# Convolution taps summed by accumulating transfers, and more seven-product chunk pairs in the up projection

## The chip, the cores and the metric

The kernel runs on one core of one Trainium2 chip. The metric is device time in microseconds: the median of three runs, 2211.19 us (2211.04 to 2212.21). The engines are TensorE (PE; PEld is its weight load), VectorE (DVE), ScalarE (ACT), GpSimd (POOL) and SyncE (SP, which here only issues transfers). Each works through its own queue in order, and they wait for each other by semaphores. Sixteen DMA engines move the data.

## The reference

Two decoder layers on one sequence of 256 tokens and width 2048 in float32; the first mixes by gated linear attention, the second by forgetting attention, and both read 256 memory tokens. Behind each mixer stands the channel mixer that this change concerns:

```python
def causal_dwconv(u, w, b):
    s_ = u.shape[1]
    up = jnp.pad(u, ((0, 0), (CONV_WIDTH - 1, 0), (0, 0)))
    return w[0] * up[:, 0:s_] + w[1] * up[:, 1:s_ + 1] + w[2] * up[:, 2:s_ + 2] + b

def conv_ffn(h, w_up, conv_w, conv_b, w_down):
    u = causal_dwconv(h @ w_up, conv_w, conv_b)
    a, val = split_cols(u, [FFN_HIDDEN, FFN_HIDDEN])
    return (jax.nn.silu(a) * val) @ w_down
...
    for i in range(DEPTH):
        ...
        h = rmsnorm(x, norm_ffn[i])
        x = x + conv_ffn(h, ffn_w_up[i], ffn_conv_w[i], ffn_conv_b[i], ffn_w_down[i])
    return rmsnorm(x, norm_final)
```

`FFN_HIDDEN` is 5632, so `w_up` is 2048 x 11264 and `w_down` 5632 x 2048; the convolution has three taps along the tokens.

## The kernel before

**Products in parts.** Every weight chunk of 128 x 1024 values is loaded as float32 (`raw`, four buffers), cast on ScalarE to a high part (`whi`, four buffers), and VectorE subtracts to get the low part (`wlo`, four buffers). The activations (`h`, in bufA and bufB) are held as two parts as well. A product is three matmuls: both activation parts with the high weights, and the high activations with the low weights. Casts and subtractions are issued with raised priority (`AHEAD`), so the scheduler, which orders all engines by a simulated time line, puts them well ahead of the matmuls.

**The channel mixer** (`ffn`). The up projection runs in 11 panels for each layer, `j` = 0, 4, ..., 40: four blocks of 128 channels of the gate half and the same four of the value half. A panel walks 16 chunks of the input dimension (`pair_steps`): four products of 128 tokens x 512 channels in a chunk, 12 matmuls of 512 columns. Two neighbouring chunks `k`, `k+1` that stand in `sums` are computed together by a scheme of seven products in place of eight, 21 matmuls in place of 24. It takes two loads into `raw2`, four sums of weight halves on VectorE (L437 to L440), and four casts and subtractions (L382, L383: one of 512 columns and three of 1024), and it uses sums over tokens of the input, prepared once a layer (`up_sums`). All panels take the pair of chunks 6 and 7. Panels whose number stands in `MORE_IN` take the pair of chunks 11 and 12 (`SEVEN_MORE`) as well: panels 5, 6 and 8. After up panels 0 to 4, 5 to 7 and 8 to 10 follow down projections (`down_pair`), of the same build.

**From panel to product.** When a panel's banks are complete, `turn` transposes its result on VectorE into `y` (tile `yu` or `yzu`), two slots to a panel. Through GpSimd's queue it is stored to DRAM (`far`, L650) and fetched back as four pieces (L655, into `fvt` or `yzu`), which brings channels onto partitions. Then for each slot: twelve ScalarE instructions scale the result by the taps' weights (`tap_of`, L1414; tap 0 with the bias), into three tiles `taps[0..2]` that both slots share; two VectorE instructions add taps 1 and 2 to tap 0 (`add_tap`, L1421); ScalarE applies SiLU in place (`silu`, L1427); VectorE multiplies gate and value (`gated`, L1434) and the product is split into parts for the down projection.

**What sets their place.** This work is cut into steps, each with a cost and a due time, in one list `waiting`. `tick` is called once for each chunk step; it gives credit (1.45 a step, 1.7 in panels of `MORE_IN`) and takes steps in order while credit lasts and they are due. A panel's results come back three ticks after its end, and its steps are due after seven or eight.

## Time and profile before

| | before |
|---|---|
| median of three runs | 2211.19 us |
| span of the profiled execution | 2210.2 us |
| own time of the profiled execution, beyond its span | not given |
| mean granted TensorE clock | 0.999 |
| first to last convolution tap, layer 0 | 517.7 to 1118.6 us |
| first to last convolution tap, layer 1 | 1556.2 to 2155.8 us |
| DMA, mean over the span | 233 GB/s |

The profile shows one execution. "Busy" is the time in which an engine works, as a share of the span. A group row reads: line, engine, operation, output<-inputs by the program's names, shapes and count | busy us, mean ns of one | idle time of the engine just before them and what ended it. Matmuls are pipelined, so the mean of one matmul is longer than the time from one to the next; the chain's time over its count is the pace.

### The profile page before, as it was taken

The numbers are of one execution on the slowest core, as the hardware profiler recorded it, in microseconds if no ns is written. First come the engines' busy times: TensorE is split into PE (matmuls) and PEld (weight loads), VectorE is DVE, ScalarE is ACT, GpSimd is POOL, SyncE is SP. The second block draws the span as 40 slices with busy tenths as digits, with TensorE's granted clock in tenths as the row PEclk, the third lists the DMA queues.
The fourth block names the chain that finished last, engine by engine and source line by source line (L and its number), as shares of the span: only waits on it lengthen the run. The fifth ranks groups of instructions, "written<-read, shape, count | busy, mean of one in ns | idle before, by whom it ended". The sixth has DMA issues, their size and how long they took to land.

```text
span 2210.2 us, 30065 instructions
## 1 busy us (share of the span) xinstructions
PE 2199.2 (100%) x10315; PEld 1851.8 (84%) x10315; DVE 1793.1 (81%) x2655; ACT 1421.8 (64%) x2260; POOL 136.5 (6%) x257
## 2 busy tenths in 40 slices
PE   9999999999999999999999999999999999999998
PEld 7888888888888888888888998888888888888886
DVE  7768977688897889888978669668888888988896
ACT  6655664566787567656865555555788656765874
POOL 0000000001100000001110000000100000100100
PEclk9999999999999999999999999999999999999999
DMA  9867567777677567667678767677777657776774
GB/s 343 259 224 224 190 194 236 252 232 253 227 243 265 187 219 233 231 234 247 222 244 265 231 201 243 225 239 241 228 241 248 234 187 237 243 247 224 227 259 153
DMA packets 166289, 515.41 MB, mean 233 GB/s; under 512 B 20780, under 2 KB 42552, under 8 KB 166136
## 3 DMA queue, kind: packets, MB, share of 16 engines
q1 hardware_dynamic: 149064, 460.99, 63.1%
q0 software_dynamic: 16496, 51.71, 7.5%
q8 instruction: 81, 1.33, 0.2%
q10 hardware_dynamic: 576, 0.79, 0.1%
q14 instruction: 72, 0.59, 0.1%
HBM read 469.62 MB, written 43.79 MB: 232 GB/s over the span
## 4 chain that ended last, share of the span: by engine, by line
PE 99%; DVE 1%; ACT 0%; issue 0%; DVEq 0%; ACTq 0%
PE acc L412 29%; PE acc L338 26%; PE ps_s L412 15%; PE ps_o L412 8%; PE ps_t L412 7%; PE acc L309 3%; PE acc L264 3%; PE ps_s L338 2%; PE acc L368 2%; PE acc L262 1%; PE ps_s L1035 0%; PE ps_o L701 0%; PE ps_s L701 0%; PE ps_s L1308 0%; PE ps_s L1081 0%; PE ps_o L1263 0%
## 5 line engine op out<-in xcount | busy, mean ns | idle before, releaser
L234 DVE TENSOR_TENSOR wlo<-raw,whi 128x1024 fp32r<-128x1024 f32 (+2 forms) x705 | 841.2, 1203 | 241.3 <-ACT whi L233 220.7
L233 ACT ACTIVATE whi<-raw 128x1024 fp32r<-128x1024 f32 (+2 forms) x705 | 729.8, 1046 | 405.4 <-PE acc L338 131.9
L338 PE MATMUL acc<-whi,B 128*128 128x512 f32 (+3 forms) x1248 | 291.7, 370 | 0.0
L382 ACT ACTIVATE whi<-raw 128x1024 fp32r<-128x1024 f32 (+1 forms) x144 | 137.0, 954 | 197.4 <-PE acc L412 75.4
L338 PEld LDWEIGHTS acc<-whi,B 128*128 128x128 f32 x1248 | 226.8, 188 | 28.1
L412 PE MATMUL acc<-whi,mix 128*128 128x512 f32 x756 | 192.9, 389 | 0.0
L412 PE MATMUL acc<-whi,B 128*128 128x512 f32 x738 | 189.8, 389 | 0.0
L383 DVE TENSOR_TENSOR wlo<-raw,whi 128x1024 fp32r<-128x1024 f32 (+1 forms) x144 | 156.2, 1089 | 40.3 <-ACT whi L382 37.2
L412 PEld LDWEIGHTS acc<-whi,mix 128*128 128x128 f32 x756 | 141.9, 188 | 29.5
L412 PEld LDWEIGHTS acc<-whi,B 128*128 128x128 f32 x738 | 138.5, 188 | 28.7
L338 PE MATMUL acc<-wlo,B 128*128 128x512 f32 (+3 forms) x624 | 158.5, 369 | 0.0
L338 PEld LDWEIGHTS acc<-wlo,B 128*128 128x128 f32 x624 | 114.5, 188 | 14.6
L1414 ACT ACTIVATE tap<-fvt,cw 128x256 f32<-128x256 f32 x264 | 123.5, 531 | 2.6 <-DMA fvt<-far 2.5
L1414 ACT ACTIVATE tap<-yzu,cw 128x256 f32<-128x256 f32 x264 | 123.5, 531 | 2.0 <-DMA yzu<-far 2.0
L1421 DVE TENSOR_TENSOR tap<-tap,tap 128x1024 f32<-128x1024 f32 x88 | 107.2, 1219 | 1.4 <-ACT tap L1414 1.0
L412 PE MATMUL ps_s<-whi,mix 128*128 128x512 f32 x386 | 106.2, 389 | 0.0
L412 PE MATMUL acc<-wlo,mix 128*128 128x512 f32 x378 | 105.6, 389 | 0.0
L412 PE MATMUL acc<-wlo,B 128*128 128x512 f32 x369 | 105.1, 389 | 0.0
L412 PE MATMUL ps_s<-whi,B 128*128 128x512 f32 x342 | 93.1, 389 | 0.0
L412 PEld LDWEIGHTS ps_s<-whi,mix 128*128 128x128 f32 x386 | 72.5, 188 | 15.0
L412 PEld LDWEIGHTS acc<-wlo,mix 128*128 128x128 f32 x378 | 70.9, 188 | 14.7
L412 PEld LDWEIGHTS acc<-wlo,B 128*128 128x128 f32 x369 | 69.3, 188 | 14.4
(502 smaller groups left out, 3866.5 us busy)
## 6 DMA issues: line engine op xcount, KB each, us to landing
raw<-wp SPq DMA_DIRECT2D x741, 512.0 KB, 4.6
fvt<-far POOLq DMA_DIRECT2D x100, 128.0 KB, 5.5
raw<-wp SPq DMA_DIRECT2D x32, 384.0 KB, 3.5
far<-yu POOLq DMA_DIRECT2D x22, 512.0 KB, 5.3
far<-yzu POOLq DMA_DIRECT2D x22, 512.0 KB, 5.3
yzu<-far POOLq DMA_DIRECT2D x88, 128.0 KB, 5.5
raw<-wp SPq DMA_DIRECT2D x24, 388.0 KB, 4.4
x<-xtok SPq DMA_DIRECT2D x8, 512.0 KB, 7.2
```

The costliest lines, as they stand in the source:

```text
L233: casts.append(S.activation(hi[:, s], raw[:, s], AF.Copy))
L234: lows.append(V.tensor_tensor(lo[:, s], raw[:, s], hi[:, s].bitcast(F32), ALU.subtract))
L262: mm = TE.matmul(acc[p][c][:, :T], w[:, s], both[:, 0, :], start=False, stop=end and j == 3)
L264: mm = TE.matmul(acc[p][c], w[:, s], both, start=u == j == 0, stop=end and j == 3)
L309: mm = TE.matmul(acc[b][:, :n], src[kcs[j] - base][:, part, b * P : (b + 1) * P], w, start=u == 0 and low == part == j == 0, stop=u == end ...
L338: mm = TE.matmul(acc[b][:, :n], src[kc - base][:, part, b * P : (b + 1) * P], ready[low][:, j * room : j * room + n], start=i == low == pa ...
L368: mm = TE.matmul(acc[b][:, :n], src[kc - base][:, part, b * P : (b + 1) * P], w, start=i == low == part == j == 0, stop=i == end and low = ...
L382: casts.append(S.activation(hi[:, :n], src, AF.Copy))
L383: lows.append(V.tensor_tensor(lo[:, :n], src, hi[:, :n].bitcast(F32), ALU.subtract))
L412: r = TE.matmul(bank[name], x, w, start=name not in begun, stop=last)
L1414: S.activation(by_run(taps[i][:, s, c, i:]), zs[slot][:, :, 2 * c + s], AF.Copy if i else AF.Identity, bias=0.0 if i else w[3], scale=w[2 ...
L1421: V.tensor_tensor(taps[0], taps[0], taps[n][:, :, :, :T], ALU.add)
```

## The change

The three tap tiles become four, two columns longer: tap 0 now has its own tile for each slot (`taps[0]` and `taps[3]`, by `summed(slot)`), while taps 1 and 2 stay shared. In panels 0 to 9 (`far`) the additions are no longer VectorE instructions but transfers on GpSimd's queue from SBUF to SBUF that add to their destination (`accum_op`), one of 128 x 1032 values each. Panel 10 adds on VectorE as before. Taps 0 and 1 are written first, then the first addition, then tap 2 and the second. SiLU and the gated product go to a second list, `rear_steps`, due `ADDED` = 4 ticks after the second addition for the transfers and at once otherwise. The transfers cost no credit. `MORE_IN` now holds nine panels, 2 to 10. The scratch for GpSimd's transfer descriptors is set to 4096 bytes a partition.

```diff
-MORE_IN = (5, 6, 8)
+MORE_IN = (2, 3, 4, 5, 6, 7, 8, 9, 10)
+ADDED = 4
+SCRATCH = 4096
...
-            taps = [fp.tile([P, 2, 2, T + i], F32, name=f"tap{i}") for i in range(3)]
-            for i in (1, 2):
-                nc.gpsimd.memset(taps[i][:, :, :, :i], 0.0)
+            taps = [fp.tile([P, 2, 2, T + 2], F32, name=f"tap{i}") for i in range(4)]
+            for i in range(4):
+                nc.gpsimd.memset(taps[i] if i in (0, 3) else taps[i][:, :, :, : T + 2 : T + 1] if i == 1 else
+                                 taps[i][:, :, :, :i], 0.0)
...
+            def summed(slot):
+                return taps[3 * slot]
+
             def tap_of(j, s, c, i, slot):
 
+                t = taps[i] if i else summed(slot)
...
-                    S.activation(by_run(taps[i][:, s, c, i:]), zs[slot][:, :, 2 * c + s], AF.Copy if i else AF.Identity,
+                    S.activation(by_run(t[:, s, c, i : T + i]), zs[slot][:, :, 2 * c + s], AF.Copy if i else AF.Identity,
...
-            def add_tap(n):
-
+            def add_tap(n, slot, far):
+
+                t = summed(slot)
+                if far:
+                    sent.append(nc.gpsimd.dma_start(flat_tap(t), flat_tap(taps[n]), accum_op=ALU.add))
+                    return
                 with tc.issue_after(lows[-1].ins):
-                    V.tensor_tensor(taps[0], taps[0], taps[n][:, :, :, :T], ALU.add)
+                    V.tensor_tensor(t[:, :, :, :T], t[:, :, :, :T], taps[n][:, :, :, :T], ALU.add)
...
-                        steps = [(0.5, lambda s=s, c=c, i=i: tap_of(j, s, c, i, slot)) for n in ((1, 2), (0,))
-                                 for s in range(2) for c in range(2) for i in n]
-                        steps += [(1.0, lambda: add_tap(1)), (1.0, lambda: add_tap(2)), (0.5, silu),
-                                  (1.0, lambda: gated(j, 0)), (0.7, lambda: gated(j, 1))]
+                        far = j < HID // P - 4
...
+                        def ended():
+                            add_tap(2, slot, far)
+                            rear_steps.extend((clock[0] + (ADDED if far else 0), *step) for step in (
+                                (0.5, lambda: silu(slot)), (1.0, lambda: gated(j, 0, slot)),
+                                (0.7, lambda: gated(j, 1, slot))))
+
+                        cost = 0.0 if far else 1.0
+                        steps = [*taps_of(0, 1), (cost, lambda: add_tap(1, slot, far)), *taps_of(2), (cost, ended)]
...
-                while waiting and waiting[0][0] <= clock[0] and credit[0] > 0:
-                    _, cost, step = waiting.pop(0)
+                while credit[0] > 0:
+                    ready = [q for q in (rear_steps, waiting) if q and q[0][0] <= clock[0]]
+                    if not ready:
+                        break
+                    _, cost, step = ready[0].pop(0)
...
-    nc = bacc.Bacc("TRN2", target_bir_lowering=False, num_devices=1)
+    nc = bacc.Bacc("TRN2", target_bir_lowering=False, num_devices=1, dynamic_dma_scratch_size=SCRATCH)
```

Three places show how instructions move. A row is line, operation, output<-inputs, shape, and how often in a row; lines of the changed kernel stand lower in its file by up to 27.

On PE, the fourth up panel of layer 0, chunks 11 and 12 (`B_108`, `B_109`) before: `acc`, `ps_o`, `ps_s` and `ps_t` are PSUM banks.

```order
L412 MATMUL ps_o<-whi,B_108 128x512 x2
L412 MATMUL ps_s<-whi,B_108 128x512 x4
L412 MATMUL ps_t<-whi,B_108 128x512 x2
L412 MATMUL ps_o<-wlo,B_108 128x512
L412 MATMUL ps_s<-wlo,B_108 128x512 x2
L412 MATMUL ps_t<-wlo,B_108 128x512
L412 MATMUL ps_o<-whi,B_109 128x512 x2
L412 MATMUL ps_s<-whi,B_109 128x512 x4
L412 MATMUL ps_t<-whi,B_109 128x512 x2
L412 MATMUL ps_o<-wlo,B_109 128x512
L412 MATMUL ps_s<-wlo,B_109 128x512 x2
L412 MATMUL ps_t<-wlo,B_109 128x512
```

The same chunks of that panel in the changed kernel, to two matmuls before the pair's end (`usum`: the sums over tokens; `B_106` is the next single chunk):

```order
L414 MATMUL acc<-whi,B_108 128x512 x2
L414 MATMUL acc<-wlo,B_108 128x512
L414 MATMUL ps_o<-whi,B_109 128x512 x2
L414 MATMUL ps_s<-whi,usum 128x512 x2
L414 MATMUL ps_o<-wlo,B_109 128x512
L414 MATMUL ps_s<-wlo,usum 128x512
L414 MATMUL acc<-whi,usum 128x512 x6
L414 MATMUL ps_s<-whi,B_109 128x512 x2
L414 MATMUL acc<-wlo,usum 128x512 x2
L414 MATMUL ps_o<-whi,B_106 128x512 x2
L414 MATMUL ps_s<-whi,B_106 128x512 x2
L414 MATMUL ps_t<-whi,B_106 128x512 x2
```

Twenty-four matmuls became 21 (19 of them in this piece, two behind it), and the pair stands ahead of chunk 9 (`B_106`). Over the program PE has 36 matmuls of 512 columns fewer; SP issues as many loads, of which 24 go to `raw2` in place of `raw`.

On GpSimd's queue in layer 0, the round trips of a panel's two slots and of the next panel's first, before (`yu_4577` is slot 1, `yu_4576` slot 0):

```order
L650 DMA far_7517<-yu_4577 128x1024
L655 DMA fvt_4571<-far_7517 32x4x256 x4
L650 DMA far_7529<-yu_4576 128x1024
L655 DMA fvt_4571<-far_7529 32x4x256 x4
L650 DMA far_7894<-yu_4577 128x1024
L655 DMA fvt_4571<-far_7894 32x4x256 x4
```

And in the changed kernel (`tap3` is slot 1's sum, `tap0` slot 0's):

```order
L652 DMA far_5743<-yu_4576 128x1024
L657 DMA fvt_4571<-far_5743 32x4x256 x4
L1429 DMA tap3_4596<-tap1_4594 128x1032
L1429 DMA tap3_4596<-tap2_4595 128x1032
L1429 DMA tap0_4593<-tap1_4594 128x1032
L1429 DMA tap0_4593<-tap2_4595 128x1032
L652 DMA far_6124<-yu_4577 128x1024
L657 DMA fvt_4571<-far_6124 32x4x256 x4
```

Four additions now stand between a panel's second fetch and the next panel's first store.

On ScalarE beside the fourth up panel of layer 0, before, the end of the third panel's slot 1: the writes of tap 0 (`tap_4593`; taps 1 and 2 are `tap_4594` and `tap_4595`) up to the SiLU (L1427), with slot 0's first write of tap 1 ahead of it:

```order
L1414 ACTIVATE tap_4593<-fvt,cw 128x4x2x32
L233 ACTIVATE whi<-raw 128x1024
L1414 ACTIVATE tap_4593<-fvt,cw 128x4x2x32 x3
L233 ACTIVATE whi<-raw 128x1024
L1509 ACTIVATE fvt<-fvt,ny 128x512
L1509 ACTIVATE temp<-temp,ny 128x512 x2
L233 ACTIVATE whi<-raw 128x1024 x3
L1414 ACTIVATE tap_4594<-fvt,cw 128x4x2x32 x2
L1427 ACTIVATE tap_4593<-tap_4593 128x2x256
```

And the same place in the changed kernel (`tap_4596` slot 1's sum, `tap_4593` slot 0's). Right ahead of this piece stand slot 1's last write of `tap_4594`, its four writes of `tap_4595` and one cast; `tap_4594` and `tap_4595` are now written for slot 0:

```order
L1421 ACTIVATE tap_4593<-fvt,cw 128x4x2x32
L235 ACTIVATE whi<-raw 128x1024
L1421 ACTIVATE tap_4593<-fvt,cw 128x4x2x32
L235 ACTIVATE whi<-raw 128x1024
L1421 ACTIVATE tap_4593<-fvt,cw 128x4x2x32 x2
L235 ACTIVATE whi<-raw 128x1024
L1421 ACTIVATE tap_4594<-fvt,cw 128x4x2x32 x4
L1536 ACTIVATE fvt<-fvt,ny 128x512
L1536 ACTIVATE temp<-temp,ny 128x512 x2
L235 ACTIVATE whi<-raw 128x1024
L1421 ACTIVATE tap_4595<-fvt,cw 128x4x2x32 x3
L1441 ACTIVATE tap_4596<-tap_4596 128x2x256
```

Slot 1's SiLU has moved behind slot 0's tap writes. The write of `tap_4594` waits until the first addition has read that tile, and the write of `tap_4595` and the SiLU wait for the second; five casts stand between slot 1's last write of `tap_4594` and these.

More of the change, by code (lines that the diff above doesn't have):

```diff
@@ L1575, in ffn @@
                 tick(2.4)
-            assert not waiting and not returns
+            assert not waiting and not returns and not rear_steps
             if l:
```

15 lines of the change are left out of this document (10 added, 5 removed).

## Prediction

> **What bounds the kernel now.** First the page's engine row and its chain that ended last, then TensorE's (PE's) own waits.
>
> ```profile
> PE 2199.2 (100%) x10315; PEld 1851.8 (84%) x10315; DVE 1793.1 (81%) x2655; ACT 1421.8 (64%) x2260; POOL 136.5 (6%) x257
> ...
> PE 99%; DVE 1%; ACT 0%; issue 0%; DVEq 0%; ACTq 0%
> ```
>
> ```profile
> PE ps_o L183 <- DVE B L180: 1.5, 1, 1.5
> PE acc L412 <- ACT whi L382: 0.7, 1, 0.7
> ```
>
> PE is busy for the whole span and waits 2.2 us in all; nothing else stands on the chain. So matmuls taken away shorten the time in full, as long as the other engines still keep ahead of PE, and nothing that relieves VectorE or ScalarE gains anything by itself. The chain in order of time prices a matmul of 512 columns:
>
> ```profile
> 885.17 32.64 PE acc L412 x144
> ```
>
> 32.64 / 144 = 0.2267 us. A chunk of 12 takes 2.72 us, and a seven-product pair of 21 takes 4.76 us. A panel with one pair is 14 × 12 + 21 = 189 matmuls, 42.84 us. The windows view agrees: the stretch between two panels' first stores is 42.81 us, all of it PE. Its columns are length, then busy time of PE, PEld, DVE, ACT and POOL (with counts), the granted clock, the DMA share and GB/s. Beside it stand the first five up panels with the down pair that begins behind them:
>
> ```profile
> 545.38:588.19 42.81, 42.81 (x191) 35.44 (x190) 37.18 (x46) 33.13 (x54) 5.46 (x11) 1.00 0.74 248
> ```
>
> ```profile
> 470.00:710.00 240.00, 240.00 (x1060) 198.74 (x1059) 204.40 (x264) 179.12 (x280) 27.36 (x50) 1.00 0.74 242
> ```
>
> The clock is 1.00 there. VectorE has 13% of that panel left, ScalarE 23%, the DMA engines 26%.
>
> **PE's term.** Six more panels in each of two layers compute chunks 11 and 12 as a pair: 21 matmuls in place of 24, so 12 × 3 = 36 go. 36 × 0.2267 = **8.2 us**. The new pairs have a price too: 36 pairs now cost PE one wait of 0.7 us, so 12 more cost about 0.2 us.
>
> **VectorE and ScalarE.** Rows by line and shape (busy, mean ns):
>
> ```profile
> L234 DVE TENSOR_TENSOR wlo<-raw,whi 128x1024 fp32r<-128x1024 f32 x667 | 806.6, 1219 | 225.3 <-ACT whi L233 207.5 <-issue 3.0 <-PE acc L262 2.7
> L233 ACT ACTIVATE whi<-raw 128x1024 fp32r<-128x1024 f32 x667 | 698.8, 1059 | 375.6 <-PE acc L338 105.5 <-PE ps_t L412 64.3 <-PE acc L412 61.1
> L383 DVE TENSOR_TENSOR wlo<-raw,whi 128x1024 fp32r<-128x1024 f32 x108 | 132.0, 1223 | 29.9 <-ACT whi L382 28.3
> L382 ACT ACTIVATE whi<-raw 128x1024 fp32r<-128x1024 f32 x108 | 114.6, 1062 | 151.7 <-PE acc L412 53.0 <-PE ps_t L412 51.6 <-DVE raw L438 30.0
> L1421 DVE TENSOR_TENSOR tap<-tap,tap 128x1024 f32<-128x1024 f32 x88 | 107.2, 1219 | 1.4 <-ACT tap L1414 1.0
> ...
> L439 DVE TENSOR_TENSOR raw<-raw,raw 128x512 f32<-128x512 f32 x36 | 24.9, 691 | 0.9
> ...
> L383 DVE TENSOR_TENSOR wlo<-raw,whi 128x512 fp32r<-128x512 f32 x36 | 24.8, 688 | 10.4 <-ACT whi L382 9.0 <-PE acc L412 1.2
> L382 ACT ACTIVATE whi<-raw 128x512 fp32r<-128x512 f32 x36 | 22.7, 631 | 45.7 <-PE acc L412 22.4 <-PE ps_t L412 12.8 <-PE ps_s L412 3.9
> ```
>
> Of 88 tap additions 80 leave VectorE: 80 × 1.219 = 97.5 us less. A pair replaces two chunks' subtractions (2 × 1.219) by three wide and one narrow (3 × 1.223 + 0.688) and four sums of weights (4 × 0.691): 4.7 us more, 56 us for 12. Net VectorE loses 41 us. ScalarE gains 3 × 1.062 + 0.631 − 2 × 1.059 = 1.7 us a pair, 20 us in all. In a panel that has both edits VectorE stays level (−4 × 1.219 + 4.7) and ScalarE goes from 33.1 to 34.8 of some 42.2 us. Neither becomes the bound, so both terms count nothing; what hides them is the idle time just named, and without it the 20 us of ScalarE would be the price.
>
> **The new transfers.** This is the unknown: no row of before shows an accumulating transfer. Nearest are GpSimd's stores of 0.5 MB, in the same stretch of 240 us, and the time to landing of all stores of that line:
>
> ```profile
> q0 software_dynamic: 3360, 10.49, 14.0%
> ...
> far<-yu POOLq DMA_DIRECT2D x10, 512.0 KB, 6.2
> ```
>
> ```profile
> DMA to landing us min/median/max: 2.7/5.0/9.5
> ```
>
> Queue 0 took 14.0% of 240 us, 33.6 us of all 16 engines, for 10.49 MB: 3.2 us per MB. One transfer adds 128 × 1032 × 4 B = 0.53 MB, so 1.7 us of the engines. For its landing time L the ends are 2.7 us (the fastest store) and 19 us (the slowest one's 9.5, paid twice, as the destination is read as well). I take the nearest row, 6.2 us, plus one more pass of the engines for that read, 1.7: **L = 7.9 us**.
>
> Who waits? The two additions of a slot go one behind the other, so the sum is complete 2L after the first can start. In six of the ten panels a layer, ScalarE has five casts between slot 1's last write of tap 1 and the next write of tap 2 and the SiLU, which need both additions (the order shown with the change tells the count, PE's pace the length): 5 × 2.72 = 13.6 us. In two panels it is 16.3 and in two 18.4. ScalarE would then wait 2 × 7.9 − 13.6 = 2.2 us in its queue, with the casts behind it, and VectorE's subtractions and PE behind those. ScalarE's waits now:
>
> ```profile
> ACT whi L233 <- DMA raw<-wp: 56.0, 48, 3.4
> ```
>
> ```profile
> ACT whi L382 <- DVE raw L438: 30.0, 13, 3.8
> ```
>
> ```profile
> 590.08 1.07 ACT L233 ACTIVATE whi<-raw 128x1024 fp32r<-128x1024 f32 x1 [1.65 <-PE ps_t L412]
> ```
>
> Waits of up to 3.8 us occur already, and PE shows 0.7 us of them. The last row is why: when the burst of tap work is over, ScalarE waits for PE to free one of four cast buffers, so it is ahead by at least two whole chunks, 5.4 us. A wait of 2.2 us stays inside that. PE idles only from 2L = 13.6 + 5.4 = 19.0, L = 9.5 us.
>
> On GpSimd's queue the next panel's store stands behind slot 0's second addition, which waits for the first to land:
>
> ```profile
> 583.42 1.57 ACT L1414 ACTIVATE tap<-fvt,cw 128x256 f32<-128x256 f32 x3
> ```
>
> ```profile
> 588.19 0.56 POOL L650 DMA_DIRECT2D far<-yu  x1 [25.06 <-DVE yu L1464]
> 594.03 2.18 POOL L655 DMA_DIRECT2D fvt<-far  x4 [5.28 <-DMA far<-yu]
> ```
>
> Tap writes end at 585.0 in the trace. The first addition can start about one chunk earlier, near 582, lands near 590, and the store goes some 2 us late; its readers are taps of the next panel, and the same 5.4 us covers them. SP's loads are as many as before; only 24 of them change their buffer. The memsets and the smaller scratch touch nothing that is late.
>
> **Sum.** The profiled span is 2210.2 us, the median of the runs 2211.19; the 1.0 us between them I leave as what lies around the span. 2210.2 + 1.0 − 8.2 + 0.2 = **2203.2 us**. A measurement of this kernel can tell about 0.2%, 4.4 us.
>
> **Rivals.** (1) *Slower: the sums land too late.* Decided at L = 9.5 us. For it: an addition reads its destination, and if all of the store's 6.2 us is paid twice, L is 12.4. Then PE idles 24.8 − 19.0 = 5.8 us in 12 panels, 3.1 in four (16.3 + 5.4) and 1.0 in four (18.4 + 5.4): 86 us, **2289 us**. Against it: landing holds parts that a second read does not double, such as the issue.
>
> (2) *Slower: the DMA engines fill.* Four additions a panel of 42.8 us are 6.8 us of the engines, 0.16; the up stage's share goes from 0.74 to 0.90. With two full passes each it is 1.06, loads fall behind by 6% of 20 panels × 42.2 us, 51 us, **2254 us**. It decides at 1.6 passes (0.26 / 0.16). The page's opening slice shows such a limit, 9 tenths at 343 GB/s:
>
> ```profile
> DMA  9867567777677567667678767677777657776774
> GB/s 343 259 224 224 190 194 236 252 232 253 227 243 265 187 219 233 231 234 247 222 244 265 231 201 243 225 239 241 228 241 248 234 187 237 243 247 224 227 259 153
> ```
>
> The Trainium skill, page "Collectives: The Full Stack", section "The bandwidth ceiling: the fold count and why AG ≠ RS ≠ AR", says that an adding transfer issues two source reads on one ring and so runs at half a copy's rate (a measured ratio of 1.93). By that rule this rival would come true, and the sum would be 2254; no run here shows an addition yet. Against it: the additions stay inside SBUF, while most of the 0.74 is weights from HBM, and demand below 0.6 in the down pairs lets the queues empty.
>
> (3) *No change: the gain is given back in places.* Landings scatter (2.7 to 9.5 for one line). With 2L near 19.3 to 20, or a few panels that lose 3 us, PE idles 4 to 12 us in all: **2207 to 2215 us**.
>
> **How the numbers follow.** The forecast gets 0.53: its gain is counted, and its cover is 1.6 us of L wide (7.9 against 9.5). Rival 3 gets 0.17, rivals 1 and 2 get 0.15 each. So faster 0.53, same 0.17, slower 0.30. The likeliest case alone runs from 2201.5 (no PE wait left) to 2206.8. The range reaches up to rival 2's 2254; with part of rival 1 it holds some 0.84, and 0.16 lies above.
>
> **What would show it.** Right: PE has 36 fewer matmuls and under 4 us of waits; VectorE near 1752 us, ScalarE near 1442; tap additions landing in 6 to 9.5 us; ScalarE waits of 2 to 3 us before tap writes or the SiLU. Wrong: landings above 9.5 us with PE waiting on casts in the up panels (rival 1), or a DMA share near 1 there with loads landing well above their 4.5 us now (rival 2; the row below):
>
> ```profile
> raw<-wp SPq DMA_DIRECT2D x91, 512.0 KB, 4.5
> ```

## The result, and the profile after

| | before | after |
|---|---|---|
| median of the runs | 2211.7 us | 2313.5 us |
| range of the runs | 2211.0 to 2212.3 | 2310.6 to 2319.6 |
| ratio | 1 | 1.0462, 95% interval 1.0450 to 1.0475 |
| span of the profiled execution | 2210.2 us | 2308.8 us |
| mean granted TensorE clock | 0.999 | 0.988 |
| PE busy / idle in the span | 2199.2 / 11.0 us | 2233.7 / 75.1 us |

The change costs 102 us where 8 us less was forecast. In the profiled executions the span grew by 98.6 us: PE idles 64.1 us more (75.1 against 11.0), and it is busy 34.5 us longer although 36 matmuls (8.2 us) are gone, so the matmuls that stayed took 42.7 us more.

From the page of after, its engine row, queue 0 and two of its DMA issues (KB each, median us to landing):

```profile
PE 2233.7 (97%) x10279; PEld 1855.5 (80%) x10279; DVE 1760.9 (76%) x2647; ACT 1438.2 (62%) x2284; POOL 211.9 (9%) x341
...
q0 software_dynamic: 28016, 93.98, 17.0%
...
tap<-tap POOLq DMA_DIRECT2D x80, 516.0 KB, 7.9
...
far<-yu POOLq DMA_DIRECT2D x22, 512.0 KB, 6.8
```

PE's 36 matmuls are gone, VectorE and ScalarE do what was forecast, and an addition lands in 7.9 us, as forecast. What changed is that PE waits. The largest of PE's waits of after (engine, line <- releaser: us in total, times, longest):

```profile
PE ps_o L414 <- ACT whi L235: 25.0, 9, 4.3
PE acc L414 <- ACT whi L235: 18.3, 9, 3.9
PE acc L414 <- ACT whi L384: 9.0, 15, 1.3
```

PE waits for ScalarE's casts of weights, both of single chunks (L235) and of pairs (L384). So ScalarE's lead over PE runs out, though ScalarE is busy for 62% of the span. Two of ScalarE's own waits:

```profile
ACT whi L384 <- DVE raw L440: 91.0, 27, 7.0
ACT tap L1421 <- DMA tap<-tap: 56.1, 16, 5.2
```

By its whole list it waits 78 us for additions (56.1 ahead of tap writes, 22.1 ahead of SiLU), 30 us for fetches ahead of tap writes (4.5 before), 98 us for loads of weights (58 before) and 105 us for VectorE's sums of weights in the pairs (39 before). How the additions hold ScalarE up is read from GpSimd's queue. In the timeline of before (start, us, engine, line, operation, count [idle before it <- what ended it]) the first store of two panels looks so:

```profile
632.42 0.56 POOL L650 DMA_DIRECT2D far<-yu  x1 [25.28 <-DVE yu L1464]
...
676.73 0.56 POOL L650 DMA_DIRECT2D far<-yu  x1 [26.39 <-DVE yu L1464]
```

GpSimd sits idle for 25 to 26 us and then stores when VectorE has the data: 44.3 us from store to store, the pace of PE. The same queue of after, one panel:

```profile
596.29 0.85 POOL L1429 DMA_DIRECT2D tap<-tap  x1 [11.01 <-ACT whi L235]
596.82 0.86 POOL L652 DMA_DIRECT2D far<-yu  x1
606.08 2.24 POOL L657 DMA_DIRECT2D fvt<-far  x4 [8.39 <-DMA far<-yu]
608.30 0.57 POOL L652 DMA_DIRECT2D far<-yu  x1
618.31 2.19 POOL L657 DMA_DIRECT2D fvt<-far  x4 [9.44 <-DMA far<-yu]
628.90 0.94 POOL L1429 DMA_DIRECT2D tap<-tap  x1 [8.41 <-ACT tap L1421]
634.64 0.88 POOL L1429 DMA_DIRECT2D tap<-tap  x1 [4.80 <-ACT whi L235]
637.62 0.86 POOL L1429 DMA_DIRECT2D tap<-tap  x1 [2.11 <-ACT tap L1421]
648.00 0.85 POOL L1429 DMA_DIRECT2D tap<-tap  x1 [9.51 <-ACT whi L235]
648.53 0.86 POOL L652 DMA_DIRECT2D far<-yu  x1
```

Read it as a loop. Store, 9.3 us until its fetch can go, second store, 10.0 us until its fetch, the taps on ScalarE, four additions spread over 19.1 us (628.90 to 648.00), and the next panel's store directly behind the last of them, with no idle time. The name in the last addition's bracket is that of a cast; what it waited for shows on ScalarE, which may write the shared tap 2 for slot 0 only when slot 1's second addition, issued at 634.64, has landed. The loop takes 51.7 us (596.82 to 648.53) where PE takes 42.8 to 44.3 for a panel, and the slack of 25 us is gone. The queue itself held this store for only 1.1 us: VectorE ended the second transpose of its data at 647.4. But VectorE, too, had stood still for the additions:

```profile
645.52 0.69 DVE L1448 TENSOR_TENSOR cv<-tap 128x512 f32<-128x512 f32 x1 [2.17 <-ACT tap L1441]
...
646.75 0.67 DVE L1478 STREAM_TRANSPOSE yu<-temp 128x512 f32<-128x512 f32 x1
```

L1448 is the gate's product of the panel before. It waits for SiLU (L1441), which on ScalarE comes right behind the tap writes that wait for the addition issued at 634.64 and needs that addition itself. The transposes of the new panel stand behind it in VectorE's queue. So the loop closes twice, through GpSimd's queue and through VectorE's, and in this stretch it is as long as the panel. ScalarE behind the fetch issued at 606.08, and behind that addition:

```profile
614.83 1.49 ACT L1421 ACTIVATE tap<-fvt,cw 128x256 f32<-128x256 f32 x3 [5.59 <-DMA fvt<-far]
...
643.66 1.30 ACT L1421 ACTIVATE tap<-fvt,cw 128x256 f32<-128x256 f32 x3 [3.55 <-DMA tap<-tap]
```

and PE behind the first of these waits:

```profile
617.32 0.74 PE L414 MATMUL ps_o<-whi,B 128*128 128x512 f32 x2 [3.32 <-ACT whi L235]
617.90 1.37 PE L414 MATMUL ps_s<-whi,B 128*128 128x512 f32 x4
619.06 1.06 PE L414 MATMUL ps_t<-whi,B 128*128 128x512 f32 x2
619.92 0.63 PE L414 MATMUL ps_o<-wlo,B 128*128 128x512 f32 x1
620.34 1.06 PE L414 MATMUL ps_s<-wlo,B 128*128 128x512 f32 x2
621.20 0.63 PE L414 MATMUL ps_t<-wlo,B 128*128 128x512 f32 x1
621.62 0.78 PE L414 MATMUL acc<-whi,B 128*128 128x512 f32 x2
```

ScalarE waits 5.59 us for the late fetch, PE waits 3.32 us for the cast behind it, and the next matmuls come at half pace: 619.06 to 619.92 is two matmuls, 0.43 us each against 0.2267, though no wait stands in these rows. From 617.32 to 621.62 twelve matmuls take 4.30 us in place of 2.72, so this wait costs PE about half as much again. Two windows of after show it in the granted clock, the seven matmuls from 619.06 on and the 40 us around them (columns: start and end, length, busy time of PE, PEld, DVE, ACT and POOL with counts, clock, DMA share, GB/s):

```profile
619.06:621.62 2.56, 2.56 (x7) 2.00 (x6) 2.50 (x5) 1.58 (x4) 1.44 (x3) 0.50 0.71 170
590.00:630.00 40.00, 34.56 (x134) 26.54 (x132) 29.95 (x42) 24.71 (x40) 7.32 (x12) 0.91 0.77 235
```

The Trainium skill, page "TensorE: Matmul & The Clock Gate", Part 1, "The HAM clock gate", states that PE falls to half its clock after an idle window of about 3.4 us and needs a busy one of about 3.4 us to come back. The trace agrees in the pace (0.43 us, at a granted clock of 0.50). The times are near the page's and not the same: an idle of 3.32 us was enough here, and one of 2.86 us ahead of 669.46 (eight matmuls in 3.34 us right behind it), and full pace was back some 4.5 us behind the first matmul at 617.32.

### The profile page after: what moved, and what is told of

Its sections match the earlier page's. It is cut to its first block, busy times and chain, and to the rows that moved or that the text cites. A ratio compares the mean times of both kernels' runs of the same rounds, so it can differ in the third digit from the quotient of the medians.

```text
span 2308.8 us, 30250 instructions
## 1 busy us (share of the span) xinstructions
PE 2233.7 (97%) x10279; PEld 1855.5 (80%) x10279; DVE 1760.9 (76%) x2647; ACT 1438.2 (62%) x2284; POOL 211.9 (9%) x341
## 5 line engine op out<-in xcount | busy, mean ns | idle before, releaser
L236 DVE TENSOR_TENSOR wlo<-raw,whi 128x1024 fp32r<-128x1024 f32 (+2 forms) x681 | 811.2, 1200 | 303.3 <-ACT whi L235 281.5
L235 ACT ACTIVATE whi<-raw 128x1024 fp32r<-128x1024 f32 (+2 forms) x681 | 703.8, 1044 | 343.8 <-PE acc L340 132.1
L384 ACT ACTIVATE whi<-raw 128x512 fp32r<-128x512 f32 x192 | 182.2, 952 | 258.8 <-DVE raw L440 91.0
L385 DVE TENSOR_TENSOR wlo<-raw,whi 128x512 fp32r<-128x512 f32 x192 | 207.8, 1085 | 62.4 <-ACT whi L384 59.4
L340 PEld LDWEIGHTS acc<-wlo,B 128*128 128x128 f32 x624 | 114.5, 188 | 14.7
L1429 POOL DMA_DIRECT2D tap<-tap x80 | 70.5, 881 | 532.4 <-ACT tap L1421 271.9
L414 PE MATMUL ps_o<-whi,mix 128*128 128x512 f32 x222 | 72.6, 402 | 14.5 <-ACT whi L235 12.6
```

What stands on the lines that cost most here:

```text
L235: casts.append(S.activation(hi[:, s], raw[:, s], AF.Copy))
L236: lows.append(V.tensor_tensor(lo[:, s], raw[:, s], hi[:, s].bitcast(F32), ALU.subtract))
L340: mm = TE.matmul(acc[b][:, :n], src[kc - base][:, part, b * P : (b + 1) * P], ready[low][:, j * room : j * room + n], start=i == low == pa ...
L384: casts.append(S.activation(hi[:, :n], src, AF.Copy))
L385: lows.append(V.tensor_tensor(lo[:, :n], src, hi[:, :n].bitcast(F32), ALU.subtract))
L414: r = TE.matmul(bank[name], x, w, start=name not in begun, stop=last)
```

## The experiments

The runs take the change apart. The theories of the expectations: A, ScalarE waits for the chain of two additions and for the stores queued behind it, and the clock falls; B (later P), the added pairs stall PE by themselves; C, the DMA engines are full; V, VectorE is behind; then R, S and H on what makes the pairs late. All ratios are to runs of the kernel before that were measured along with the run. The runs with more tiles also give the descriptor scratch another size (3840 bytes, in pairs_raw2 4096).

| run | additions | pairs | median us | ratio (95%) |
|---|---|---|---|---|
| acc_only | transfers | three panels | 2266.5 | 1.0251 (1.0231 to 1.0271) |
| before_pairs | VectorE, kernel before | nine | 2247.5 | 1.0162 (1.0145 to 1.0179) |
| pairs_dve | VectorE | nine | 2249.7 | 1.0174 (1.0159 to 1.0189) |
| pairs_none | none | nine | 2242.5 | 1.0137 (1.0122 to 1.0152) |
| pairs_no_sums | none, and no weight sums | nine | 2214.8 | 1.0016 (1.0006 to 1.0025) |
| pairs_place | VectorE, first pair not moved | nine | 2261.8 | 1.0228 (1.0213 to 1.0243) |
| pairs_raw2 | VectorE, four buffers | nine | 2250.3 | 1.0176 (1.0160 to 1.0191) |
| pairs_none_raw2 | none, four buffers | nine | 2247.0 | 1.0156 (1.0139 to 1.0173) |
| one_far | tap 1 VectorE, tap 2 transfer | nine | 2249.7 | 1.0171 (1.0156 to 1.0186) |
| one_far_raw2 | the same, four buffers | nine | 2251.0 | 1.0183 (1.0168 to 1.0198) |
| no_chain | transfers, no chain | nine | 2285.1 | 1.0332 (1.0308 to 1.0356) |
| acc_no_chain | transfers, no chain | three | 2232.8 | 1.0094 (1.0079 to 1.0109) |
| acc_own_taps | transfers, own tap tiles | three | 2263.4 | 1.0241 (1.0224 to 1.0258) |
| acc_late_silu | the same, SiLU later | three | 2271.6 | 1.0276 (1.0261 to 1.0291) |
| acc_silu_free | the same, SiLU not waiting | three | 2247.1 | 1.0163 (1.0148 to 1.0178) |
| acc_plain | plain copies, own tap tiles | three | 2222.5 | 1.0052 (1.0037 to 1.0067) |
| after_plain | plain copies | nine | 2260.5 | 1.0218 (1.0201 to 1.0235) |
| after_no_sums | transfers, no weight sums | nine | 2301.2 | 1.0401 (1.0375 to 1.0427) |

### Which edit costs what

**acc_only**: the transfers with the old pairs.

```diff
-MORE_IN = (2, 3, 4, 5, 6, 7, 8, 9, 10)
+MORE_IN = (5, 6, 8)
```

> The changed kernel with the second pair back in panels 5, 6 and 8 only; the additions stay transfers. Theory A (waits on the additions: ScalarE stalls at the second addition's landing and at fetches whose store stood behind that addition on GpSimd's queue, PE idles and its clock drops behind each stall): nearly all of the loss stays, PE waits of 45 us or more, 2300 to 2325 us (8 us more matmuls than the changed kernel). Theory B (the added pairs stall PE at their own casts, the waits of PE on L384): most of the loss goes, under 2260 us. Theory C (the DMA engines are full): as A.

**pairs_dve**: the changed code with every addition on VectorE.

```diff
-                        far = j < HID // P - 4
+                        far = False
```

> The changed kernel with every addition on VectorE (no accumulating transfer), nine panels with two pairs, and the new order of the steps. Theory A and theory C: the loss goes and the pairs' gain shows, PE waits under 5 us, 2203 to 2208 us. Theory B: PE waits on casts of pairs (L384) stay at some 19 us and more, 2225 us or more.

**before_pairs**: the kernel before with nine panels of two pairs.

```diff
-MORE_IN = (5, 6, 8)
+MORE_IN = (2, 3, 4, 5, 6, 7, 8, 9, 10)
```

> The kernel before with nine panels of two pairs and nothing else. Theory A and C: 2203 to 2210 us, a gain cut by some waits because VectorE keeps its tap additions (37.7 us busy of 40 in such a panel before). Theory B: 2215 us or more, with PE waiting on casts of pairs.

Each edit alone is slower than before: the transfers by 55 us (2266.5, between the bands of A and B), the pairs by 37 to 39 us (2247.5 and 2249.7, as theory B expects). These add up to 92 to 94 of the 102 us. Neither edit gains anything, and the two mechanisms can be looked for apart.

**pairs_none**: the change with no addition at all in panels 0 to 9.

```diff
                 if far:
-                    sent.append(nc.gpsimd.dma_start(flat_tap(t), flat_tap(taps[n]), accum_op=ALU.add))
                     return
```

> The changed kernel with neither transfers nor VectorE additions of taps in panels 0 to 9 (taps 1 and 2 are left out there); nine panels with two pairs. Theory V (nine panels with VectorE's additions stall because VectorE is behind, and ScalarE's SiLU waits for it ahead of the pair's casts): 2203 to 2208 us, PE waits under 5 us. Theory P (the second pair itself is late: its loads wait for the first pair's two buffers, and its casts for VectorE's four sums, whatever the additions do): 2225 us or more, PE waiting on the pairs' casts.

**one_far**: one addition on VectorE, the other by a transfer.

```diff
-                        steps = [*taps_of(0, 1), (cost, lambda: add_tap(1, slot, far)), *taps_of(2), (cost, ended)]
+                        steps = [*taps_of(0, 1), (1.0, lambda: add_tap(1, slot, False)), *taps_of(2), (cost, ended)]
```

> The changed kernel with tap 1 added on VectorE and only tap 2 by a transfer: half the transfers, no chain of two, and no wait of GpSimd's queue for a landing. Theory A: the waits on additions go; what is left is VectorE's 49 us more work, 2215 to 2260 us. Theory C: half of the transfers' loss stays, 2270 us or so.

With nobody adding, the pairs still cost 31 us over before (2242.5, theory P), 39 us over the forecast. VectorE's additions put 5 to 7 us on top of it (2247.5 and 2249.7). With one transfer a slot in place of two the time is 2249.7, as in pairs_dve: a single addition by transfer, which doesn't stand behind another, costs no more that shows than the VectorE addition that it replaces.

### What makes the transfers cost 55 us

**no_chain** and **acc_no_chain**: the second transfer adds into a tile that nobody reads, with nine and with three panels of two pairs (tap 2 is left out of the sums of panels 0 to 9).

```diff
-                    sent.append(nc.gpsimd.dma_start(flat_tap(t), flat_tap(taps[n]), accum_op=ALU.add))
+                    to = t if n == 1 else spill
+                    sent.append(nc.gpsimd.dma_start(flat_tap(to), flat_tap(taps[n]), accum_op=ALU.add))
```

> The changed kernel, but the second transfer of each slot adds to a spill tile, so that it waits for no first addition and the SiLU waits for the first alone (tap 2 is left out of the sum in panels 0 to 9). As many accumulating transfers of the same size. Theory A: the waits on additions and the late stores go, PE waits under 10 us, 2203 to 2215 us. Theory C: the DMA engines carry the same load, so most of the loss stays, 2270 us or more. Theory B: 2225 us or more.

> Second pairs in panels 5, 6 and 8 only; the second transfer of each slot adds to a spill tile and waits for no first one (tap 2 is left out of the sum in panels 0 to 9). Transfers as many and as large as in the run with additions alone, 2266 us. Theory A (the waits on the chain of two additions): 2211 to 2220 us. Theory C (the load on the DMA engines): 2245 us or more, loads of weights landing in 5 us or more.

Same traffic, same queue, but the second addition of a slot doesn't wait for the first, and SiLU waits for the first alone: 28 us come back in the changed kernel, 34 of 55 us with the old pairs. What stays is 21 us with the old pairs (2232.8, between the bands of A and C) and 43 us over pairs_none in the changed kernel (2285.1, in the band of C). So theory C can't be dropped: the traffic costs something by itself, and beside the pairs twice as much.

**acc_own_taps**: with the old pairs, taps 1 and 2 have tiles of their own for each slot (the additions read them accordingly).

```diff
-            taps = [fp.tile([P, 2, 2, T + 2], F32, name=f"tap{i}") for i in range(4)]
+            taps = [fp.tile([P, 2, 2, T + 2], F32, name=f"tap{i}") for i in range(6)]
...
-                t = taps[i] if i else summed(slot)
+                t = taps[3 * slot + i]
```

> Second pairs in panels 5, 6 and 8 only, additions by transfers, and own tiles for taps 1 and 2 in each slot, so that no tap write waits for the other slot's transfers. Theory A: ScalarE's 53 us of waits of tap writes on transfers go and PE's waits halve, 2225 to 2250 us; what is left are the SiLUs and the stores behind the second addition. Theory C: 2260 us or more, unchanged.

It gains 3 us (the intervals of the two ratios overlap), which is the band of C and not of A: ScalarE's wait for a tap tile that an addition still reads was not the cost with the old pairs. GpSimd's queue of this run, at the end of a panel:

```profile
679.42 0.84 POOL L1430 DMA_DIRECT2D tap<-tap  x1 [8.55 <-issue]
679.96 0.86 POOL L652 DMA_DIRECT2D far<-yu  x1
689.07 2.23 POOL L657 DMA_DIRECT2D fvt<-far  x4 [8.25 <-DMA far<-yu]
691.29 0.56 POOL L652 DMA_DIRECT2D far<-yu  x1
699.88 2.18 POOL L657 DMA_DIRECT2D fvt<-far  x4 [8.03 <-DMA far<-yu]
```

and ScalarE and PE behind it:

```profile
697.73 3.67 ACT L1422 ACTIVATE tap<-fvt,cw 128x256 f32<-128x256 f32 x8 [7.11 <-DMA fvt<-far]
```

```profile
703.01 1.22 PE L414 MATMUL ps_o<-whi,mix 128*128 128x512 f32 x2 [6.87 <-ACT whi L235]
```

The idle time ahead of a panel's first store is 5.06 us at 548.08, then 2.38 at 592.22, 0.95 at 636.87 and none at 679.96. The queue loses a little in each panel; only in the fourth does PE run dry, and then for 6.87 us at once and at half pace behind it. Late loads had a part in it: at 687.02 ScalarE had just waited 4.09 us for weights. But the load on the DMA engines alone doesn't stop PE. In the two windows ahead of this one, 590 to 630 and 630 to 670, their share is 0.93 and PE is never idle; the first:

```profile
590.00:630.00 40.00, 40.00 (x179) 33.11 (x178) 31.56 (x42) 29.49 (x47) 8.23 (x13) 1.00 0.93 285
```

**acc_late_silu**: SiLU eight steps behind the second addition (in later panels it then comes behind the next panel's first taps in the same tile, so that sums of two panels are mixed).

```diff
-ADDED = 4
+ADDED = 8
```

> acc_own_taps (the transfers with the old pairs, 2263.4 us) with SiLU queued eight steps after the second addition's step in place of four. If ScalarE's wait at SiLU for the chain of two additions (58.9 us in 19 waits in acc_own_taps) is what the transfers cost: that wait falls under 10 us and the time to that of acc_no_chain or below, 2212 to 2235 us. If it is the load of the extra traffic or the clock, no change: 2255 to 2268 us.

**acc_silu_free**: SiLU and the gate read tap 1's tile, the queue is unchanged.

```diff
-                t = summed(slot)[:, :, 0, :T]
+                t = taps[3 * slot + far][:, :, 0, :T]
...
```

> acc_own_taps (the transfers with the old pairs, 2263.4 us) in which SiLU and the gate product of the ten panels read tap 1's tile in place of the sum, so that nothing on ScalarE or VectorE waits for the chain; GpSimd's queue holds the same additions, in the same order. If SiLU's wait for the sum is the cost (58.9 us in 19 waits): as acc_no_chain, 2228 to 2240 us. If it is GpSimd's queue (a second addition waits 8.5 us for the first, the next panel's two stores and fetches stand behind it, and the turned panel comes back late): 2252 to 2268 us, with ScalarE's first taps waiting for the fetch.

Moving SiLU gains nothing (2271.6, above both bands). Its wait for the sum falls from 58.9 to 16.6 us, but ScalarE now waits longer for the panel that comes back over GpSimd's queue (24 us in acc_own_taps, here 44) and for loads of weights (84.6 us at single chunks there, here 121.5). ScalarE's waits of acc_late_silu:

```profile
ACT tap L1422 <- DMA yzu<-far: 26.6, 7, 6.6
ACT tap L1422 <- DMA fvt<-far: 17.7, 4, 9.1
```

With SiLU set free altogether the time is 2247.1 us, between the two bands expected. So SiLU's and the gate's wait is worth 16 us of the 52 that acc_own_taps loses. 35 remain, with a queue that nobody waits for except through its stores and fetches and with the load on the DMA engines: ScalarE waits 26 us for the round trip at its taps and 133 us for weights (58 before). These two are not separated. In acc_no_chain, where ScalarE waits 140 us for weights and no second addition for the first, 21 us are lost.

**acc_plain**: the same transfers as plain copies.

```diff
-                    sent.append(nc.gpsimd.dma_start(flat_tap(t), flat_tap(taps[3 * slot + n]), accum_op=ALU.add))
+                    sent.append(nc.gpsimd.dma_start(flat_tap(t), flat_tap(taps[3 * slot + n])))
```

> acc_own_taps with the same transfers as plain copies (the sum's tile is overwritten, so the sums are wrong). If adding costs a second read at the target: landing falls from 7.9 to about 6.2 to 6.8 us, the DMA share of the stretch from 0.92 to about 0.83, and the chain of two is 2 to 3 us shorter: 2225 to 2250 us. If a transfer in GpSimd's queue costs the same with or without adding: 2255 to 2270 us.

This is the sharpest of the runs: same instructions, same queue, same chain, same bytes (only the issue is shorter, 0.55 against 0.87 us), and 41 of 52 us are gone (2222.5, a little better than the band). From the page of acc_own_taps:

```profile
q0 software_dynamic: 28016, 93.98, 17.2%
...
tap<-tap POOLq DMA_DIRECT2D x80, 516.0 KB, 7.6
...
far<-yu POOLq DMA_DIRECT2D x22, 512.0 KB, 7.4
```

and of acc_plain:

```profile
q0 software_dynamic: 28016, 93.98, 12.4%
...
tap<-tap POOLq DMA_DIRECT2D x80, 516.0 KB, 5.8
...
far<-yu POOLq DMA_DIRECT2D x22, 512.0 KB, 6.1
```

Queue 0 took 7.5% of 2210.2 us before, 166 us of the 16 engines. With the copies it is 12.4% of 2220.7, 275 us; with additions 17.2% of 2259.9, 389 us. If the other transfers of the queue take their 166 us in all three, the 42.3 MB cost 110 us as copies and 223 us as additions, 2.03 times as much for the same packets. The Trainium skill, page "Collectives: The Full Stack", section "The bandwidth ceiling: the fold count and why AG ≠ RS ≠ AR", gives a reduce-scatter, whose transfers add, half the rate of an all-gather, whose transfers copy; that is measured on a ring over links, and the ratio of engine time of a local addition here agrees. The landing time grows only from 5.8 to 7.6 us, so part of it doesn't double, but the stores in the same queue land later too (7.4 against 6.1), and each panel's loop holds four of the one and two of the other. The copies leave GpSimd 2.85 to 6.47 us idle ahead of the panel's first store in three panels and 0.60 in the fourth: enough.

### What makes the pairs cost 39 us

**pairs_raw2**, **pairs_none_raw2**, **one_far_raw2**: four buffers for a pair's two weight tiles, in before_pairs, pairs_none and one_far.

```diff
-                    ra, rb = [pool.tile([P, NUNIT], F32, name="raw2", tag="raw2", bufs=2) for _ in range(2)]
+                    ra, rb = [pool.tile([P, NUNIT], F32, name="raw2", tag="raw2", bufs=4) for _ in range(2)]
...
```

> The kernel before with two pairs in nine panels (no transfer of taps), as in before_pairs (2247.5 us), but with four buffers for a pair's two weight tiles in place of two. Theory R (the second pair's weights can't be fetched until the first pair's tiles are split and summed: SP waited 153.2 us in 36 waits at the pair's loads in before_pairs, 64.6 in 16 in the kernel before): the wait goes, the second pair is as early as the first, 2203 to 2212 us. Theory S (VectorE's four subtractions and low halves of two pairs within a few chunks are late, whatever the buffers: ScalarE waited 55 us for VectorE's second subtraction in before_pairs): no gain, 2240 to 2250 us.

> pairs_none (the change without any addition of taps in panels 0 to 9, taps 1 and 2 left out; 2242.5 us) with four buffers for a pair's weight tiles. VectorE has here no additions of taps at all. R: 2203 to 2210 us. S: 2236 to 2244 us.

> one_far (the change with tap 1 added on VectorE and only tap 2 by a transfer, 2249.7 us) with four buffers for a pair's weight tiles. R: the second pair's lateness goes and one transfer without a chain stays: 2205 to 2222 us. S: 2244 to 2252 us.

None gains (2250.3, 2247.0, 2251.0 against 2247.5, 2242.5, 2249.7; in or up to 3 us above the bands of S). In pairs_raw2 SP's wait of 153 us at the pair's loads falls to 2.5 us, and nothing gets faster, so theory R falls: the fetch of the second pair was never what was late.

**pairs_place**: before_pairs with the first pair where it stood before.

```diff
-                                  count[2] % 2, pool, early, late, 2 * second)
+                                  count[2] % 2, pool, early, late, 0)
```

> before_pairs (2247.5 us) with the first pair of a panel left in its old place: the plan no longer moves it two chunks forward when there is a second pair. Theory H (moved forward, the pair's subtractions fall into the time in which VectorE still evacuates the panel before and gates it, 584 to 599 us in pairs_none without a gap): 2205 to 2225 us. If the place doesn't matter: 2240 to 2255 us.

Slower still, 2261.8, above both bands: moving the first pair forward, as the kernel does, is the better place. H falls.

**pairs_no_sums**: pairs_none without VectorE's four subtractions of weights in the 36 pairs of the nine panels.

```diff
-                    V.tensor_tensor(ra[:, :512], ra[:, 512:], ra[:, :512], ALU.subtract)
-                    V.tensor_tensor(ra[:, 512:], rb[:, 512:], ra[:, 512:], ALU.subtract)
-                    V.tensor_tensor(rb[:, 512:], rb[:, 512:], ra[:, :512], ALU.subtract)
-                    summed = V.tensor_tensor(rb[:, :512], rb[:, :512], rb[:, 512:], ALU.subtract)
+                    if not ahead:
...
```

> pairs_none (no additions of taps in panels 0 to 9; 2242.5 us) with VectorE's four subtractions of weights left out in the pairs of the nine panels, so that the third and fourth split of a pair take the fetched tiles as they are. 36 pairs lose 4 x 0.68 us each, 98 us of VectorE, and ScalarE's casts no longer wait for them (104.6 us in 26 waits in pairs_none). Theory S (a pair's subtractions come late on VectorE, ScalarE stands behind them and what it would cast next is late): 2196 to 2212 us. If the pairs are late for another reason (their fetches, ScalarE's own two casts more): 2235 us or above.

28 of the 31 us that pairs_none loses are gone (2214.8, at 1.0016 three us over before and above the band by as much). The run leaves out the subtractions of all 36 pairs, and 24 of these pairs stand in the kernel before as well, so it does not price those of the 12 new pairs alone. Still it is the subtractions that the casts wait for, though VectorE is less busy in pairs_none (1758.9 us) than before (1793.1). How they hurt shows in the timeline of pairs_none, VectorE first:

```profile
592.84 0.70 DVE L1477 STREAM_TRANSPOSE yu<-fvt 128x512 f32<-128x512 f32 x1
593.47 0.65 DVE L385 TENSOR_TENSOR wlo<-raw,whi 128x512 fp32r<-128x512 f32 x1
...
594.70 1.22 DVE L385 TENSOR_TENSOR wlo<-raw,whi 128x1024 fp32r<-128x1024 f32 x1
595.84 0.68 DVE L439 TENSOR_TENSOR raw<-raw 128x512 f32<-128x512 f32 x1
...
596.64 0.68 DVE L440 TENSOR_TENSOR raw<-raw,raw 128x512 f32<-128x512 f32 x1
```

then ScalarE and PE:

```profile
597.44 1.06 ACT L384 ACTIVATE whi<-raw 128x1024 fp32r<-128x1024 f32 x1 [6.24 <-DVE raw L440]
```

```profile
598.56 1.21 PE L414 MATMUL acc<-whi,usum 128*128 128x512 f32 x4 [0.18 <-ACT whi L384]
```

VectorE comes out of the panel's end (transposes, gate products, splits) without a gap, and the subtractions stand behind all of it. ScalarE's third cast of the pair needs the second subtraction, and every later cast stands behind that cast: 6.24 us in which ScalarE does nothing, and its whole lead is gone. PE then takes each cast as it comes.

### Both in the changed kernel

**after_plain** takes only the adding out of the changed kernel, **after_no_sums** only the subtractions of the 36 pairs (the edits are those of acc_plain and pairs_no_sums).

> The changed kernel with the same transfers as plain copies in place of accumulating ones (the sums are overwritten, so they are wrong). With the old pairs the adding cost 2263.4 - 2222.5 = 41 us. If it costs the same on top of the pairs: 2313.5 - 41 = 2272 us, with the DMA engines' share of queue 0 at 12 to 12.5% instead of 17.0%, and what is left over the kernel before is the pairs (+39 to 46 less the copies' 11). If adding is dearer where the pairs have eaten the lead: 2250 to 2262 us.

> The changed kernel with VectorE's four subtractions of weights left out in the nine panels' pairs (products wrong). Without the additions the subtractions were worth 2242.5 - 2214.8 = 28 us. If the two losses add up: 2313.5 - 28 = 2285 us. If they share the same lead, so that each is dearer beside the other: 2262 to 2278 us, near acc_own_taps (2263).

Without the adding 53 us come back (2260.5, in the band in which adding is dearer beside the pairs). Without the subtractions only 12 (2301.2), in neither band. GpSimd's stores in after_no_sums:

```profile
595.20 0.56 POOL L654 DMA_DIRECT2D far<-yu  x1
...
646.52 0.56 POOL L654 DMA_DIRECT2D far<-yu  x1 [3.13 <-DVE yu L1480]
...
697.58 0.56 POOL L654 DMA_DIRECT2D far<-yu  x1 [3.48 <-DVE yu L1480]
```

51 us from store to store in this stretch, as in the changed kernel. Two of these stores waited 3 us for VectorE, so here the additions did not hold them in the queue: the panel itself came late. ScalarE's waits tell what it was late for: 66 us for additions and 54 us for fetches, against 78 and 30 in the changed kernel, while those for sums of weights fall from 105 to 21. So casts that come earlier are of little use as long as the transfers keep ScalarE waiting as much as before. That is read from the waits; no run shows it apart. Why the panels are 51 us apart here and 44 in acc_own_taps, which has the same additions, isn't settled. The shared tap tiles don't make it by themselves: acc_only has them, with the old pairs, and its stores (548.15 to 683.47) are 43.1 to 46.4 us apart. The chunks' order differs with the pairs, and in both stretches some panels have store, fetch, store, fetch (two landings one behind the other) where others have both stores first. No run changed only that.

Put together, the changed kernel's 102 us are 31 for the pairs (pairs_none), some 43 for the transfers without the chain (no_chain over pairs_none) and 28 for the chain. Of the transfers' 71 us, 53 are the adding. How much of the 43 is the load on the DMA engines, and how much the longer landings in GpSimd's queue, is open.

No version made here beats the kernel before.

## Why the prediction was wrong

**Right.** PE's count: 10279 matmuls against 10315. VectorE at 1760.9 us (forecast near 1752) and ScalarE at 1438.2 (near 1442). The landing of an addition: 7.9 us in the median, the forecast's L to the tenth, and the second pass of the engines by which it was estimated is real (acc_own_taps against acc_plain: 1.8 us of landing, 2.03 times the engine time of a copy). Single additions landed in 4.6 to 12.0 us.

**The step that failed first** is the one on GpSimd's queue: "the store goes some 2 us late; its readers are taps of the next panel, and the same 5.4 us covers them". The delay was about right: the stores at 596.82 and 648.53 went 2.3 and 1.1 us after their data were turned. What failed is the claim that the lead covers it. The delay was taken once, but store, fetch, taps, additions and the next store form a loop through one queue in order, and the question was whether the loop still fits into a panel. The prediction quoted the slack itself, 25.06 us of idle time ahead of the store. Four additions, each second one behind the landing of the first, take 19 us of it, and the later landings of stores (6.8 us against 5.3) and fetches and the waits for taps take the rest. In acc_own_taps the loop just misses a panel and PE runs dry in the fourth; in the change it takes 51.7 us. So a lead covers a delay that comes once and not one that comes in every panel. The loop is read from the rows, and the runs without the chain (34 of 55 us) and with copies (41 of 52) agree with it; no run moved the additions to another queue.

**The step on ScalarE's wait** (rival 1 rests on it) had the right landing and the wrong price. By it PE idles only from L = 9.5; L was 7.9, rival 1 was not decided by its own point, and the time came out above even that rival's 2289. SiLU's wait is worth 16 us with the old pairs (acc_silu_free), although 2 x 7.9 - 13.6 = 2.2 us was to stay inside the lead. In the change ScalarE's 21 waits for additions are 3.7 us long in the mean, up to 5.7.

**"36 pairs now cost PE one wait of 0.7 us, so 12 more cost about 0.2 us"** failed on the pairs: 31 us over before without any addition. It took the mean price of the pairs that were there, counted the four subtractions as busy time, and did not ask where they stand in VectorE's queue; 28 us go when the subtractions of all 36 pairs of these panels go (pairs_no_sums). That VectorE gets lighter in sum says nothing about the few microseconds behind a panel's end.

**The lead of 5.4 us was used for everything.** It was read in the kernel before, where ScalarE is held back by PE. The additions' waits, the late fetches and the pairs' waits all draw on it in the same panels. That they cost more together is shown only in part: the two edits alone cost 55 and 37 to 39 us, together 102, and the adding costs 53 us beside the new pairs against 41 beside the old, but the subtractions cost 12 us beside the transfers against 28 without.

**A term that was missing** is PE's pace behind a wait: the prediction priced a wait at its length. 42.7 of the 98.6 us are matmuls that run longer. The granted clock explains some 25 us of it by an estimate (0.999 less 0.988, times the span of 2308.8), most plainly the half pace behind the longer waits. It isn't all: in pairs_none the clock is 0.999, and the matmuls still run 15 us longer than in the kernel before (2206.4 us busy with 36 fewer, against 2199.2).

**Rival 2** held in part. Its load was mis-sized: the sum gives an addition 1.7 us of the engines, one pass, though L has two; it measured 2.8 us (223 / 80), which is 1.6 passes of 1.7 and just the point at which this rival was to decide. With the chain taken out, the traffic costs 21 us with the old pairs (acc_no_chain) and 43 us over pairs_none with the new ones (no_chain). Against it stands that PE kept its pace at a DMA share of 0.93 (acc_own_taps), and that the same bytes as copies cost 11 us with the old pairs. In the change the share is 0.77 from 590 to 630, where PE did the fewest matmuls, but 0.94 from 630 to 670 and 1.00 from 710 to 750, where it lost as well; what the load is worth there is open.

**Rival 3** named the scatter of the landings, which is there (4.6 to 12.0 us, past the 9.5 of the decision), and priced it at 4 to 12 us. No run shows the scatter apart. One slip hangs on nothing: 2201.5 as the time with no PE wait left should be 2203.2 - 0.2 - 2.2 = 2200.8.

## What to carry to other kernels

When work moves onto a queue that also carries a round trip, add up the loop through that queue (issue, landing, the engine behind it, the next issue) and hold it against the period of the stage; a lead covers what comes once, slack in the loop what comes each time. Price an accumulating transfer at two passes of the DMA engines, and count what else lands later beside it. An engine that is idle for a quarter of the time can still be the one that is late: look at what stands ahead of the one instruction that the next engine needs.

## What the runs showed of the hardware

- An accumulating transfer of 0.53 MB from SBUF to SBUF took 2.03 times the engine time of a plain copy (223 against 110 us of 16 engines for 80 of them) and landed in 7.6 us against 5.8. Issuing it kept GpSimd 0.87 us, a copy 0.55.
- After an idle of 3.32 us matmuls of 512 columns came every 0.29 us for 1.7 us, then every 0.42 to 0.43 us for some 3 us (granted clock 0.50 from 619.06 to 621.62), then at 0.23 again. After 6.87 us (at 703.01, in acc_own_taps) half pace was there at once and stayed for some 5 us; after 2.86 us (at 669.46) at once, for some 3 us. After 2.42 us (at 646.49) the pace stayed full.
- PE did its full number of matmuls through 80 us in which the DMA engines were busy for 93% of the time (acc_own_taps, 590 to 670).
